# Twelve projection pairs by seven products instead of nine, with plain pairs taken one channel tile at a time

## The chip, the cores and the metric

The kernel runs on one core of one Trainium2 chip. The core has a matmul engine (PE, with its weight loads listed as PEld), VectorE (DVE), ScalarE (ACT), GpSimd (POOL) and SyncE (SP), which here only issues transfers. The metric is the device time of one execution in microseconds. Before the change the median of 3 runs is 2563.29 us (2563.03 to 2566.54).

## What is computed

One layer of a bidirectional encoder on 1024 prompt tokens and 256 sample tokens with model width 2048:

```
h = rmsnorm(x, norm_w)
proj = h @ w_in                       # 9232 columns
na_q, na_k, na_v, na_g, ml_qk, ml_v, ml_o, ml_z, ml_gp = split(proj)
att = neighbourhood_attention(na_q, na_k, na_v, na_rpb) * silu(na_g)   # 8 heads of 128
qk  = silu(centred_depthwise_conv(ml_qk, conv_w, conv_b))
h   = bidirectional_mlstm(*split(qk), ml_v, ml_gp + gate_b)            # 4 heads of 256
mem = rmsnorm(h, head_norm_w) * sigmoid(ml_o) * silu(ml_z)
y   = rmsnorm(x + concat(att, mem) @ w_out, final_norm_w)
```

All of it is float32. The kernel keeps that precision with three matmuls for each product: both operands are split into a high and a low part (ScalarE writes the high part, VectorE the difference), and high times high, high times low and low times high are added up in PSUM.

## The kernel before

**Tokens and channels.** The 1280 tokens fall into group A (768) and group B (512, half of them the sample's). The projection's channels are counted in tiles of 128; two neighbouring tiles are a *pair*, named by its first tile: q is 0 to 7 (`QT0`), k 8 to 15 (`KT0`), the attention's gate 16 to 23 (`GT0`), the mLSTM's q and k 24 to 39 (`QK0`), its output gate 40 to 47 (`OT0`), its z gate 48 to 55 (`ZT0`), and from 56 on v in eight units. The inner dimension has 16 blocks of 128.

**Stage one** (from 0 to about 1097 us) does every pair for group A. `first_tiles` takes tiles 0 to 3 plainly; then `pair_a` goes through the list `order` (lines 591 to 594), which begins with pairs 4 and 6. Each pair is a product of 2x2 blocks by Strassen's seven products in Winograd's form, 168 matmuls of 384 columns. GpSimd makes four sums of weight blocks for it (`summed`, line 512), and for a pair in `SECOND` these sums are also written to a scratch tensor `sD` (line 526), 16 writes of 128 KB. While a pair's matmuls run, `bg` is stepped: the end of the pair before (`finish_a`), which scales, splits, convolves or applies a tanh and stores.

**Stage two** begins with v units 4 and 0 and plain pair 0 for group B. Then `pair_s` (line 1342) does the nine pairs in `SECOND` by seven products for group B: 168 matmuls of 256 columns (line 1379), with the four sums read back from `sD`. All other pairs of group B are done by `proj_pair` (line 650): 96 matmuls of 512 columns (line 662) over two PSUM banks at once, in four steps of one 512 KB load, two splits and 24 matmuls; and v by `proj_v` (line 718), 192 matmuls of 256 columns (line 740) into two banks, or four "a" banks for unit 4.

**Attention and mLSTM** are written as generators. `run` steps two streams in turn at high priority: the mLSTM's units and, for each head, `na_sample`, then `na_prompt` with a setup and four blocks. The plain pairs and v units, listed ahead of it in the code at ordinary priority, and then four `late_gate` calls (two pairs each, for output gate and z gate) supply matmuls in between. What each head reads (`qS`, `kS`, `vS`) goes through scratch tensors in HBM, so a head can start only when its q, k and v have been projected and stored.

**The order on each engine** is made when the program is built: a list scheduler with a simulated timeline takes instructions by priority and readiness and hands out buffers of a ring in turn. On the chip each engine then runs its list in that order, so an instruction whose operand is late holds up all that follow it on its engine. SP's queue of transfers is such a list as well.

**Rings that the change touches.** PSUM has eight banks: three under the tag "pr", five under "a" (`bank`, line 73). In SBUF, `na_sample` loads a sample's q and k into the tile "nqk" (line 797), of which there is one and which `na_prompt`'s setup also uses for 2 MB of a prompt's q and k (lines 844 and 845); "hf" is a ring of eight that holds the mLSTM's operands (line 764); "sml" is a ring of six (line 770).

**The output stage** begins when the mixed heads are in HBM: 32 loads of 320 KB (`mix_block`, line 1492, on GpSimd's queue) go into SBUF that attention's pool gave back, and seven products in each of two halves give the output.

Of the kernel before, what the change touches and what calls it, by code (L numbers as in the profile page):

```python
# [8 lines left out]
F32 = mybir.dt.float32  # L9
F32R = mybir.dt.float32r  # L10
# [28 lines left out]
    GT0, QK0 + 8, GT0 + 2, QK0, KT0, GT0 + 4, KT0 + 2, GT0 + 6, KT0 + 4,  # L39
)  # L40
# [5 lines left out]
def kernel(  # L46
# [26 lines left out]
    def bank(tag, name):  # L73
        return ps.tile([P, 512], F32, tag=tag, name=name, bufs=3 if tag == "pr" else 5)
# [207 lines left out]
    def first_tiles():  # L282
        names = ("pr", "pr", "pr", "a", "a", "a", "a", "a")
# [184 lines left out]
    def pair_a(n1, bg=iter(()), hook=None):  # L468
        nm = f"A{n1}"
        tags = ("pr", "pr", "pr", "a", "a", "a", "a")  # L470
# [120 lines left out]
    order = [4, 6]  # L591
    rest = list(range(KT0, QK0, 2)) + list(range(OT0, NCH, 2))
# [57 lines left out]
    def proj_pair(n1, X, late=False):  # L650
        pb = [bank("pr", f"pc{n1}_{j}") for j in range(2)]
        for r in range(4):
            raw = w_piece(w_in[n1 // 2, r], f"{n1}_{r}")
            t = [w_split(raw, j * 512, j * 512 + 512, f"{n1}_{r}{j}") for j in range(2)]
            for f_ in range(2):
                for q in range(2):
                    xs = X.get(8 * f_ + 2 * r + q)
                    c = (2 * f_ + q) * P
                    first, last = r + f_ + q == 0, r == 3 and f_ == 1 and q == 1
                    for j, passes in enumerate((FORTH, FORTH[::-1])):  # L660
                        for m, (wi, xi) in enumerate(passes):
                            PE.matmul(  # L662
                                pb[j], t[j][:, wi, c : c + P], xs[xi],
                                start=first and m == 0, stop=last and m == 2,
                            )
        out = []
        for j in range(2):
            o = po(f"pco{n1}_{j}")
            if QK0 <= n1 < OT0:
                ct = n1 - QK0 + j  # L670
                DM.dma_start(o[:, 0:4], qb[ct])
                for z in (260, 518):
# [3 lines left out]
                    pb[j].rearrange("p (s c) -> p s c", s=2),  # L676
# [6 lines left out]
            out_scaled(o, pb[j], rbs[1], n1)  # L683
# [25 lines left out]
    def proj_v(u, X):  # L709
# [54 lines left out]
    def sml(name, n=256, dt=F32):  # L764
        return ap.tile([P, 260], dt, tag="sml", name=name, bufs=6)[:, :n]
# [29 lines left out]
    def na_sample(h):  # L795
        nm = f"nas{h}"
        qk = na_tile("nqk", [P, 4, TP], f"{nm}qk", 1, F32R)[:, :, :TS]
# [26 lines left out]
        b = bank("a", f"{nm}o")  # L824
# [625 lines left out]
    for i, n in enumerate(SECOND):  # L1450
        bg = pair_s(n, ("pr", "a")[i % 2], bg)
# [328 lines left out]
```

## Time and profile before

| | us |
|---|---|
| median of 3 runs | 2563.29 |
| the profiled execution, own time | 2565.18 |
| its span | 2563.3 |
| mean granted clock of the matmul engine | 0.997 |
| stage one | about 0 to 1097 |
| seven-product pairs of stage two | 1173 to 1350 |
| attention, mLSTM, plain pairs | 1350 to 2114 |
| plain pairs alone | 2114 to 2160 |
| output stage | 2160 to 2563 |

How to read the profile: every time is in microseconds from the start of the span unless it is marked ns. A row of busy times names engine, time, share and number of instructions. A row of waits names who waited at which line, for whom, for how long in total, how often, and the longest. A row of the chain names start, duration, engine, tile and line; "L662 x158" is 158 instructions of line 662 in one piece. A row of a group of instructions names line, engine, operation, tile written from tiles read, shape and count, then busy time and mean ns of one, then idle time of the engine ahead of them and what ended it. In a row of a single tile the three numbers are shortest, median and longest duration in ns, followed by first and last start. Names have their numbers left out where they differ only by them: "nap3qk" is the q and k of head 3's prompt, "nas3qk" those of its sample, "S32bx" a PSUM bank of seven-product pair 32 and "pc" one of a plain pair. "busy" of the matmul engine is modelled: matmuls overlap, so a mean duration is longer than the step from one start to the next.

### The profile page before, as it was taken

To read this page: it belongs to the slowest core of one execution; us is meant where nothing else is said; L and a number is where in the kernel's file an instruction comes from. 1 tells how busy PE (TensorE), PEld (TensorE's weight loads), DVE (VectorE), ACT (ScalarE), POOL (GpSimd) and SP (SyncE) were. 2 spreads that over 40 slices of the span, in tenths; PEclk is the share of its full clock that TensorE was granted. 3 is DMA by queue.
4 is the path that set the end of the run, shared out by engine and by line. 5 is a ranking of instruction groups with operands and counts; after the bars stand their busy time and mean duration, and the time that the engine had idled before them with its cause. 6 is when DMAs were issued, how large, how long until landed. Compare 5 with 4: busy or idle time off the path is not lost.

```text
span 2563.3 us, 44540 instructions
## 1 busy us (share of the span) xinstructions
PE 2534.0 (99%) x15054; PEld 2368.6 (92%) x15054; DVE 1972.6 (77%) x4029; ACT 1345.0 (52%) x3041; POOL 615.3 (24%) x909
## 2 busy tenths in 40 slices
PE   8999999999999999999999999999999999999998
PEld 8999999999999999999999999998988887788886
DVE  8769888888869798898875866765855665879695
ACT  8535545444444444465655666655745543344444
POOL 0535555444544444410001110100100104000001
PEclk9999999999999999999999999999999999999999
DMA  6546464536434342467768878877867849636237
GB/s 215 174 143 200 143 199 130 179 124 200 125 112 126 101 141 89 154 228 223 239 223 299 297 243 272 293 234 261 286 197 251 277 126 377 202 125 218 85 87 254
DMA packets 303483, 503.03 MB, mean 196 GB/s; under 512 B 48752, under 2 KB 191256, under 8 KB 303256
## 3 DMA queue, kind: packets, MB, share of 16 engines
q1 hardware_dynamic: 299096, 484.46, 58.9%
q0 software_dynamic: 4160, 15.73, 1.6%
q8 instruction: 119, 1.95, 0.3%
q14 instruction: 108, 0.88, 0.1%
HBM read 373.13 MB, written 126.95 MB: 195 GB/s over the span
## 4 chain that ended last, share of the span: by engine, by line
PE 92%; DMA 5%; DVE 2%; issue 1%; ACT 1%; SPq 0%; POOL 0%; ACTq 0%; POOLq 0%; DVEq 0%
PE pc L662 16%; PE po L1613 14%; PE pv L740 5%; PE fb L274 2%; PE A24b L274 1%; PE A12b L274 1%; PE A16b L274 1%; PE A44b L274 1%; PE A48b L274 1%; PE A52b L274 1%; PE A40b L274 1%; PE A20b L274 1%; PE A8b L274 1%; PE A50b L274 1%; PE A42b L274 1%; PE A22b L274 1%
## 5 line engine op out<-in xcount | busy, mean ns | idle before, releaser
L1613 PE MATMUL po<-wo,mo 128*128 128x512 f32 x1620 | 376.9, 393 | 3.7 <-ACT wo L165 2.8
L1613 PEld LDWEIGHTS po<-wo,mo 128*128 128x128 f32 x1620 | 303.6, 188 | 76.2 <-ACT wo L165 4.2
L166 DVE TENSOR_TENSOR ws<-wr,ws 128x512 fp32r<-128x512 f32 x152 | 104.3, 696 | 53.2 <-ACT ws L165 52.4
L165 ACT CAST ws<-wr 128x512 fp32r<-128x512 f32 x152 | 92.5, 617 | 70.1 <-PE pc L662 57.5
L165 ACT CAST mo<-mb 128x640 fp32r<-128x640 f32 x72 | 51.8, 726 | 92.5 <-PE po L1613 73.7
L116 POOL TENSOR_SCALAR rs<-rs 128x1 f32<-128x1 f32 x10 | 3.4, 341 | 351.2 <-DVE rs L1593 351.1
L166 DVE TENSOR_TENSOR mo<-mb,mo 128x640 fp32r<-128x640 f32 x72 | 59.1, 827 | 27.1 <-ACT mo L165 27.0
L1562 DVE TENSOR_TENSOR y<-y,po 128x512 f32<-128x512 f32 x90 | 58.5, 687 | 11.3 <-PE po L1613 11.0
L165 ACT CAST mo<-ms 128x640 fp32r<-128x640 f32 x40 | 28.9, 726 | 61.1 <-PE po L1613 32.1
L166 DVE TENSOR_TENSOR wsv<-wr_v,wsv 128x512 fp32r<-128x512 f32 x64 | 44.4, 700 | 14.2 <-ACT wsv L165 13.9
L165 ACT CAST wsv<-wr_v 128x512 fp32r<-128x512 f32 x64 | 39.0, 617 | 26.8 <-PE pv L740 15.5
L1576 ACT ACTIVATE jk<-y 128x512 f32<-128x512 f32 x40 | 25.2, 631 | 36.5 <-DVE y L1562 36.2
L413 DVE SCALAR_TENSOR_TENSOR pcv<-pco,cw_sb,pcv 128x516 f32<-128x516 f32 x48 | 36.7, 764 | 7.1 <-ACT pcv L407 7.0
L166 DVE TENSOR_TENSOR mo<-ms,mo 128x640 fp32r<-128x640 f32 x40 | 32.8, 823 | 7.6 <-ACT mo L165 7.6
L129 ACT ACTIVATE xq<-xq 128x1024 f32<-128x1024 f32 x20 | 21.2, 1061 | 31.7 <-DMA xq<-in_xtok_dram 29.2
L1081 POOL MEMSET mls_0v<- 128x2 f32 x4 | 0.4, 102 | 145.1 <-DVE S_dt.float L166 119.7
L274 PE MATMUL fb<-xg,fw 128*128 128x384 f32 x192 | 34.6, 334 | 0.0
L251 DVE TENSOR_TENSOR pco<-pc,rstdb 128x512 f32<-128x512 f32 x30 | 20.6, 687 | 17.8 <-PE pc L662 17.1
L274 PEld LDWEIGHTS fb<-xg,fw 128*128 128x128 f32 x192 | 33.4, 188 | 0.0
L778 DVE CUSTOM_DVE_ANT_0 nap_0st<-nap_0s,nap_0bt 128x384 f32<-128x384 f32 x32 | 17.7, 555 | 20.1 <-PE nap_0s L773 8.7
L1525 DVE TENSOR_TENSOR ms<-mb,mb 128x640 f32<-128x640 f32 x40 | 32.8, 823 | 0.0
L1492 POOL DMA_DIRECT2D mb<-mx x32 | 17.7, 554 | 58.8 <-DVE ws L166 24.8
(2655 smaller groups left out, 8512.4 us busy)
## 6 DMA issues: line engine op xcount, KB each, us to landing
wr<-in_w_in_dram SPq DMA_DIRECT2D x76, 512.0 KB, 4.7
wr_v<-in_w_in_dram SPq DMA_DIRECT2D x32, 512.0 KB, 5.0
wb<-in_w_o_dram SPq DMA_DIRECT2D x48, 256.0 KB, 3.0
xq<-in_xtok_dram SPq DMA_DIRECT2D x20, 512.0 KB, 4.2
mb<-mx POOLq DMA_DIRECT2D x32, 320.0 KB, 8.2
wr_wp<-in_w_o_dram SPq DMA_DIRECT2D x16, 512.0 KB, 4.0
vS<-vo SPq DMA_DIRECT2D x24, 256.0 KB, 5.1
nap_0bt<-in_rpb_tab_dram SPq DMA_DIRECT2D x32, 192.0 KB, 4.3
```

The costliest lines, as they stand in the source:

```text
L129: S.activation(raw, raw, AF.Square, accum_out=ssq[g][:, t, q : q + 1])
L165: S.copy(hi, src)
L166: V.tensor_tensor(lo, src, f(hi), op=ALU.subtract)
L251: V.tensor_tensor(o, src, rb, op=ALU.mult)
L274: PE.matmul(o, w(a_), x(b_), start=first and m == 0, stop=last and m == 2)
L413: V.scalar_tensor_tensor(dst[:, a:n], src[:, a + j - pad : n + j - pad], cw_sb[:, ct, j : j + 1], dst[:, a:n], op0=ALU.mult, op1=ALU.add,)
L662: PE.matmul(pb[j], t[j][:, wi, c : c + P], xs[xi], start=first and m == 0, stop=last and m == 2,)
L740: PE.matmul(outs[tt], xs[:, tt * P : (tt + 1) * P], t[:, wi, q * w : (q + 1) * w], start=first and m == 0 and (gates or tt % 2 == 0), stop ...
L1525: V.tensor_tensor(t, x, y_, op=op)
L1562: V.tensor_tensor(Y[p, q, tt], Y[p, q, tt], bk, op=op)
L1576: S.activation(jk, Y[p, q, tt], AF.Square, accum_out=ss[t][:, c : c + 1])
L1613: PE.matmul(bk[tt], m[xi][:, tt * P : (tt + 1) * P], w[wi], start=first and kk == 0 and j == 0, stop=last and j == 2, skip_group_check=True,)
```

## The change

Three more pairs are added to `SECOND`: k pair 14 and q pairs 4 and 6. They are thereby spilled in stage one, done by `pair_s` in stage two, and left out of the plain pairs.

```diff
 SECOND = (
     GT0, QK0 + 8, GT0 + 2, QK0, KT0, GT0 + 4, KT0 + 2, GT0 + 6, KT0 + 4,
+    KT0 + 6, QT0 + 4, QT0 + 6,
 )
```

Stage one opens with two output-gate pairs (40, 42); pairs 4 and 6 come to the head of the rest, which are dealt out two at a time behind an mLSTM pair and a v pair.

```diff
-    order = [4, 6]
-    rest = list(range(KT0, QK0, 2)) + list(range(OT0, NCH, 2))
+    order = [OT0, OT0 + 2]
+    rest = [4, 6] + list(range(KT0, QK0, 2)) + list(range(OT0 + 4, NCH, 2))
```

One of the three "pr" banks becomes a bank "m". It serves where the third "pr" bank served in `first_tiles`, `pair_a`, `pair_s` and the output stage, takes the first tile of plain pair 0, and holds the outputs of attention, which were in the "a" ring.

```diff
-        return ps.tile([P, 512], F32, tag=tag, name=name, bufs=3 if tag == "pr" else 5)
+        return ps.tile([P, 512], F32, tag=tag, name=name, bufs={"pr": 2, "m": 1, "a": 5}[tag])
...
-        bg = pair_s(n, ("pr", "a")[i % 2], bg)
+        bg = pair_s(n, (("pr", "pr", "m"), ("a", "a", "a"))[i % 2], bg)
...
-        b = bank("a", f"{nm}o")
+        b = bank("m", f"{nm}o")
...
-            b = bank("a", f"{n2}o")
+            b = bank("m", f"{n2}o")
```

A plain pair runs through the whole inner dimension for its first channel tile, scales and stores it, and then does the second. A load brings the weights of one tile for two of the four steps.

```diff
     def proj_pair(n1, X, late=False):
-        pb = [bank("pr", f"pc{n1}_{j}") for j in range(2)]
-        for r in range(4):
-            raw = w_piece(w_in[n1 // 2, r], f"{n1}_{r}")
-            t = [w_split(raw, j * 512, j * 512 + 512, f"{n1}_{r}{j}") for j in range(2)]
...
         out = []
         for j in range(2):
+            pb = bank("m" if n1 + j == QT0 else "pr", f"pc{n1}_{j}")
+            for r in range(4):
+                if r % 2 == 0:
+                    raw = w_piece(
+                        w_in[n1 // 2, r : r + 2, :, j * 512 : (j + 1) * 512].rearrange(
+                            "r p c -> p r c"
+                        ),
+                        f"{n1}_{j}{r}",
+                    )
+                t = w_split(raw, r % 2 * 512, r % 2 * 512 + 512, f"{n1}_{j}{r}")
+                for fq in range(4):
+                    f_, q = divmod(fq, 2)
+                    xs = X.get(8 * f_ + 2 * r + q)
+                    first, last = r + fq == 0, r + fq == 6
+                    for m, (wi, xi) in enumerate(FORTH[:: (1, -1)[fq % 2]]):
+                        PE.matmul(
+                            pb, t[:, wi, fq * P : fq * P + P], xs[xi],
+                            start=first and m == 0, stop=last and m == 2,
+                        )
             o = po(f"pco{n1}_{j}")
```

The v units' splits out of PSUM get high priority. In attention and mLSTM, a sample's q and k come into a buffer of the ring "hf", "sml" has seven buffers, and the throw-away output of the squares has a buffer of its own.

```diff
-            store_v(u, GA + tt * P, o, outs[tt][:, :256], rc[:, tt : tt + 1])
+            with tc.high_priority():
+                store_v(u, GA + tt * P, o, outs[tt][:, :256], rc[:, tt : tt + 1])
...
-        return ap.tile([P, 260], dt, tag="sml", name=name, bufs=6)[:, :n]
+        return ap.tile([P, 260], dt, tag="sml", name=name, bufs=7)[:, :n]
...
-        qk = na_tile("nqk", [P, 4, TP], f"{nm}qk", 1, F32R)[:, :, :TS]
+        qk = hf(f"{nm}qk")[:, : 4 * TS].rearrange("p (i c) -> p i c", i=4)
...
-                jk = sml(f"{n2}jk{e}")
+                jk = ap.tile([P, 256], F32, tag="jk", name=f"{n2}jk{e}", bufs=1)
```

More of the change, by code (lines that the diff above doesn't have):

```diff
@@ L650, in proj_pair @@
     def proj_pair(n1, X, late=False):
-        pb = [bank("pr", f"pc{n1}_{j}") for j in range(2)]
-        for r in range(4):
-            raw = w_piece(w_in[n1 // 2, r], f"{n1}_{r}")
-            t = [w_split(raw, j * 512, j * 512 + 512, f"{n1}_{r}{j}") for j in range(2)]
[L655 to L665, printed above, removed]
         out = []
         for j in range(2):
+            pb = bank("m" if n1 + j == QT0 else "pr", f"pc{n1}_{j}")
[17 more added lines that the diff above has]
+                        )
             o = po(f"pco{n1}_{j}")
@@ L1340, with pair_s @@
     BLOCK = {1: 0, 2: 1, 4: 3}
-    def pair_s(n1, tag, bg):
+    def pair_s(n1, tags, bg):
         nm = f"S{n1}"
-        bx, by, bz = (bank(tag, f"{nm}b{i}") for i in "xyz")
+        bx, by, bz = (bank(t, f"{nm}b{i}") for t, i in zip(tags, "xyz"))
         x0, y0, z0, y1, z1 = bx[:, :256], by[:, :256], bz[:, :256], by[:, 256:], bz[:, 256:]
@@ L1644, in product @@
             each(tt)
-    slots = iter(("aaaaa" "ppp") * 8)
+    slots = iter((("a",) * 5 + ("pr", "pr", "m")) * 8)
     def p_banks(p, j):
-        return [bank("pr" if next(slots) == "p" else "a", f"po{p}_{j}_{i}") for i in range(NT)]
+        return [bank(next(slots), f"po{p}_{j}_{i}") for i in range(NT)]
     for i in range(4):
```

8 lines of the change are left out of this document (4 added, 4 removed).

## The prediction

> **What bounds the kernel now.** I read the page's busy times first, then the waits of the matmul engine, then busy times by stretch, and for the terms of the sum the chain in order of time.
>
> ```profile
> span 2563.3 us, 44540 instructions
> PE 2534.0 (99%) x15054; PEld 2368.6 (92%) x15054; DVE 1972.6 (77%) x4029; ACT 1345.0 (52%) x3041; POOL 615.3 (24%) x909
> ```
>
> The matmul engine is busy for all but 29.3 us. So an edit counts if it shortens the stream of matmuls or one of the few places where that stream stands still. Those are, waits first and then stretches (columns: PE, PEld, DVE, ACT and POOL busy, granted clock, DMA share, GB/s):
>
> ```profile
> PE fb L274 <- ACT fw L172: 7.1, 1, 7.1
> PE nap_0s L773 <- DMA nap3qk<-kS: 2.5, 1, 2.5
> PE nap_0s L773 <- DMA nap4qk<-kS: 1.9, 1, 1.9
> PE A4b L274 <- DVE A4s L173: 1.7, 1, 1.7
> PE A6b L274 <- ACT A4c L483: 1.5, 1, 1.5
> PE nap_0s L773 <- DMA nap2qk<-kS: 0.5, 1, 0.5
> ```
>
> ```profile
> 1173.00:1350.00 177.00, 177.00 (x1538) 176.50 (x1537) 140.26 (x274) 105.54 (x203) 0.39 (x6) 1.00 0.72 227
> 1350.00:2113.60 763.60, 758.49 (x4833) 687.75 (x4832) 513.20 (x1396) 448.57 (x1114) 68.59 (x252) 1.00 0.78 254
> 2113.60:2160.20 46.60, 46.60 (x202) 37.77 (x202) 25.38 (x39) 15.20 (x25) 20.11 (x37) 1.00 0.94 364
> 2160.20:2201.00 40.80, 37.09 (x156) 28.59 (x154) 27.68 (x42) 12.61 (x21) 8.53 (x16) 1.00 0.89 325
> ```
>
> The first stretch is the nine seven-product pairs of stage two; the second is attention and mLSTM with plain pairs between their matmuls; the third is plain pairs alone; the fourth is the start of the output stage, where 3.7 us are lost.
>
> **Three more seven-product pairs.** From the chain in order of time (start, us, what):
>
> ```profile
> 1195.47 2.84 PE S32bx L1379 x24
> 1234.05 2.84 PE S24bx L1379 x24
> ...
> 1892.00 36.60 PE pc L662 x158
> ...
> 2101.31 6.11 PE pc L662 x26
> ...
> 2113.64 39.53 PE pc L662 x170
> ```
>
> Two pairs by seven products, 32 and 18, lie between 1195.47 and 1234.05: 19.29 us each. A plain matmul takes 36.60/158 = 0.2316 or 39.53/170 = 0.2325 us; 96 of 0.232 make 22.27 us. Three pairs move from the second form to the first: 3 x (22.27 - 19.29) = **8.9 us** less on the engine that sets the end. The break-even pace of a 256-column matmul is 22.27/168 = 0.133 us; the rows show 19.29/168 = 0.115.
>
> The Trainium skill, TensorE: Matmul & The Clock Gate, Back-to-back issue gap, speaks against narrow products: it gives a sustained pace of about 131 ns at 512 columns and 81 ns at 128, from which I estimate some 98 ns at 256, so 16.4 us for seven products against 12.6 us plain, and three pairs would cost 12 us. The trace's 0.232 us at 512 columns contradicts this; the same section's isolated gap (N/2.4 + 2.5 ns) would make the saving 7.1 us.
>
> Each moved pair needs 14 splits of 128x512 in stage two instead of 8, and its sums and folds beside them:
>
> ```profile
> L166 DVE TENSOR_TENSOR ws<-wr,ws 128x512 fp32r<-128x512 f32 x152 | 104.3, 696 | 53.2 <-ACT ws L165 52.4
> L165 ACT CAST ws<-wr 128x512 fp32r<-128x512 f32 x152 | 92.5, 617 | 70.1 <-PE pc L662 57.5
> ```
>
> That is 6 x 0.696 = 4.2 us more for VectorE and 6 x 0.617 = 3.7 us more for ScalarE per pair, in a stretch where VectorE has 36.7 of 177 us free and the matmul engine shows none. The two q pairs also write 256-byte runs from there instead of later; as many packets as before, and the DMA share is 0.72. Cost nothing; without that cover 3 x 4.2 = 12.6 us at most.
>
> The pairs' operand sums are spilled in stage one: 16 writes per pair on the SP queue, each waiting for GpSimd's sum, with the next weight load and the stores of the pair before queued behind it.
>
> ```profile
> 211.48 9.36 PE A8b L274 x54
> 271.21 29.13 PE A26b L274 x168
> 801.56 9.36 PE A44b L274 x54
> 861.29 29.13 PE A36b L274 x168
> sD<-A8t SPq DMA_DIRECT2D x16, 128.0 KB, 2.2
> ```
>
> Pairs 8 and 10 spill and split k: 271.21 - 211.48 = 59.73 us. Pairs 44 and 46 do neither: 861.29 - 801.56 = 59.73 us. So 48 more spills cost nothing, and pairs 4 and 6 where 40 and 42 stood cost nothing either, their stores being of the kind that 8 and 10 make.
>
> **The opening.** Pairs 40 and 42 take the place of 4 and 6. The two waits there (1.7 and 1.5 us) are for the splits of the opening's own tiles and for the copy that follows, and those stay. Zero, between -3.2 and 0; the lighter end of pair 40 (a tanh in place, two stores) gives no reason for a loss.
>
> **Plain pairs one tile at a time, and the PSUM banks.** 96 matmuls, 8 splits and 4 loads per pair, as before; a load now brings two runs of 2 KB for a partition instead of one of 4 KB, and feeds 24 matmuls as before.
>
> ```profile
> wr<-in_w_in_dram SPq DMA_DIRECT2D x76, 512.0 KB, 4.7
> L251 DVE TENSOR_TENSOR pco<-pc,rstdb 128x512 f32<-128x512 f32 x30 | 20.6, 687 | 17.8 <-PE pc L662 17.1 <-DMA mlp_2k<-cS 0.7
> L168 ACT ACTIVATE vo<-pv,rstdc x32: 454/472/505, 1120.5 to 1862.3; 128x256 fp32r<-128x256 f32 x32
> L169 DVE SCALAR_TENSOR_TENSOR vo<-pv,rstdc,vo x32: 462/481/491, 1122.7 to 1863.7; 128x256 fp32r<-128x256 f32 x32
> ```
>
> A bank lasts half a pair, 11 us, and is emptied in 0.69 us beside the next one's matmuls. With two "pr" banks instead of three the tight place is behind a v unit: it holds both, and the next unit's first matmul waits until two tiles have been split out of the older one, 2 x (0.472 + 0.481) = 1.9 us, covered by the v unit's last 12 matmuls and by attention. Six v units in the second stretch: 0 to 11.4 us; I take 1, since attention's matmuls stand next in the engine's order and the change gives these splits priority.
>
> **Sample q and k from the other ring.** Now a sample's q and k use the only buffer of the prompt's. Head 3:
>
> ```profile
> L773 PE MATMUL nap_1s<-nap2qk x12: 334/335/342, 1555.2 to 1595.3; 128*128 128x384 f32 x12
> L799 SPq DMA_DIRECT2D nas3qk<-kS x1: 606/606/606, 1596.2 to 1596.2; - x1
> L773 PE MATMUL nas_1s<-nas3qk x3: 274/277/279, 1619.5 to 1619.7; 128*128 128x256 f32 x3
> L845 SPq DMA_DIRECT2D nap3qk<-kS x1: 602/602/602, 1624.0 to 1624.0; - x1
> L773 PE MATMUL nap_0s<-nap3qk x12: 333/337/421, 1634.4 to 1688.1; 128*128 128x384 f32 x12
> ```
>
> The prompt's last score ends at 1595.3, the sample's load goes out at 1596.2, its scores end at 1619.7, and only then, at 1624.0, goes the next prompt's load, for which the matmul engine stands until 1634.4. After the change that load can go out 27.8 us sooner, behind the last score of the prompt before, and 10.4 us are all it took. The three waits (2.5 + 1.9 + 0.5 = 4.9 us) lose their cause, and so does what follows two of them:
>
> ```profile
> 1634.40:1640.00 5.60, 5.60 (x32) 5.56 (x33) 4.00 (x12) 2.13 (x7) 1.77 (x6) 0.70 1.06 385
> 1734.00:1740.00 6.00, 6.00 (x35) 6.00 (x36) 3.33 (x11) 2.84 (x9) 0.60 (x1) 0.72 0.97 330
> ```
>
> The granted clock is 0.70 and 0.72 there: 0.30 x 5.6 + 0.28 x 6.0 = 3.4 us. Together 8.3; I take **6**, since the order of matmuls is laid down ahead by a planner and another load can be the late one (bounds -8.3 and 0).
> The Trainium skill, same page, Part 1 on the clock gate, has the clock halve after an idle window of about 3.4 us; here waits of 2.5 and 1.9 us were enough, so by the page's figure the term would be at most 4.9 instead of 8.3, and the rows decide.
>
> The sample takes one of the eight "hf" buffers of the mLSTM for about 20 us per head; bounded by nothing (a free one) and the mLSTM's next unit 20 us later, hidden as long as plain pairs remain. One more "sml" and a buffer of its own for the squares' output only loosen. The single "m" bank for attention's outputs leaves all five "a" banks to the rest.
>
> **What is late next.** The second stretch loses 66.8 us of plain matmuls, and attention must still end ahead of them. Today it ends at 2113.6 and 46.6 us of plain pairs follow. Attention lost about 30 us at 1892 (158 plain matmuls in a row take 36.6 us, where a stretch like the one at 2101 has 6), waiting for the last q and k pairs; and
>
> ```profile
> L799 SPq DMA_DIRECT2D nas4qk<-kS x1: 567/567/567, 1691.4 to 1691.4; - x1
> L799 SPq DMA_DIRECT2D nas4qk<-qS x1: 524/524/524, 1714.6 to 1714.6; - x1
> ```
>
> head 4's q came 23.2 us after its k, from a plain pair as well. All three pairs involved (4, 6, 14) are then done before attention starts. Without any shortening of the heads, attention takes 763.6 - 30 = 734 us of the 763.6 + 46.6 - 66.8 = 743 that the engine needs; with 10 us less in each of seven heads, some 664. So the matmul engine stays the bound, and about 80 us of plain pairs follow attention. Then the output stage's loads, whose start is set by attention's end, are further along when the stage begins: the 3.7 us lost there shrink to nothing or, with no lead left (46.6 us more of the same loss, 3.71/40.8 each), grow by 4.2. I take -1.
>
> **Sum**, against the profiled execution's own time, 2565.2 us (span 2563.3 and 1.9 around it): -8.9 - 6 + 1 - 1 = -14.9, so 2550.3. That execution lies 1.9 us above the median of the three runs, 2563.3, so a median near **2548**.
>
> **The rivals.** (a) The products are saved and the waits come back elsewhere: other loads late, clock dips with them. For it: the transfers run at a DMA share of 1.0 and the planner did not foresee them. Against: the shared buffer is gone. 2563.3 - 8.9 = 2554. (b) What is won is lost at the banks and at the output stage, both terms at their bad ends: -8.9 - 6 + 11.4 + 4.2 = +0.7, so 2564. For it: a bank less for the plain pairs. Against: no wait for a bank among the matmul engine's waits today. (c) Attention ends last. It decides from the point where it takes over 743 us. Held up 5% by the "hf" ring it shares and the one "m" bank: 734 + 37 = 771, so 28 us of idle engine, and 4.2 more in the output stage: 2563.3 - 8.9 + 28 + 4 = 2586, **slower**. For it: only 9 us to spare if the heads get no shorter. Against: the load that ended each head's pause moves ahead by 28 us. (d) Narrow products run at the break-even pace or worse: no gain from them, 2557 with the other terms. Against: every row of the stretch.
>
> **How the numbers follow.** Forecast 0.61 (its own range 2541 to 2552), (a) 0.20, (b) 0.08, (c) 0.09, (d) 0.02. What a measurement of this kernel can tell from no change is 0.2%, 5.1 us: faster is below 2558.2. The forecast and (a), with half of (d), give faster 0.82; (b) and the rest of (d) same 0.09; (c) slower 0.09. The low end has every term at its good bound, -8.9 - 8.3 - 3.2 - 3.7 = -24.1, so 2539; the high end takes in (a) and the milder half of (b), 2562.
>
> **What would show it.** Seven-product pairs every 19.3 us, twelve times; no wait of the matmul engine for a prompt's q and k; the granted clock at 1.00 from 1400 to 2150; plain matmuls alone for more than 46.6 us before the output stage; its start without the 3.7 us. I am wrong if the matmul engine idles ahead of attention's last units, if waits stand behind v units, or if stage one's pairs exceed 59.7 us for two.

## The result, and the profile after

The changed kernel takes 2572.09 us (median of 7 runs, 2567.87 to 2577.93), the kernel before on the same chip 2562.7 us (7 runs, 2559.49 to 2566.54): ratio 1.0039, 95% interval 1.0028 to 1.0050. It is slower by 0.39%; 2548 was forecast, and the range ended at 2562.

The profiled execution after took 2572.09 us itself; that of before lies 2.5 us above the median of this comparison. The head of the page, and the waits of the matmul engine (us in total, times, longest):

```profile
span 2570.4 us, 45222 instructions
PE 2533.5 (99%) x15270; PEld 2376.0 (92%) x15270; DVE 1989.5 (77%) x4062; ACT 1353.2 (53%) x3071; POOL 611.1 (24%) x909
```

```profile
PE fb L275 <- ACT fw L173: 6.9, 1, 6.9
PE mlp0a3tb L1126 <- DMA mlp0a3cv<-cD: 2.3, 1, 2.3
PE mlp3a2kv L1101 <- POOL mlp3a0v L1089: 2.3, 1, 2.3
...
PE mls_0s L1101 <- DMA mls_0q<-cS: 2.0, 2, 1.8
...
PE pc L669 <- DVE vo L170: 1.2, 1, 1.2
PE mlp_3in L1101 <- DVE mlp_1zr L1286: 1.2, 1, 1.2
```

The three waits for a prompt's q and k are gone, and there is a longer list in their place; behind the first row no single wait is longer than 2.3 us. The stretches (the columns as in the prediction):

```profile
1176.40:1411.00 234.60, 234.60 (x2041) 234.16 (x2040) 181.19 (x347) 137.61 (x266) 0.26 (x4) 1.00 0.73 227
1411.00:1450.00 39.00, 34.08 (x248) 32.23 (x247) 16.68 (x52) 15.88 (x43) 5.49 (x27) 0.91 0.98 312
1905.00:1940.00 35.00, 29.22 (x206) 27.09 (x206) 22.15 (x67) 17.70 (x50) 2.97 (x15) 0.95 0.82 259
1411.00:2079.40 668.40, 653.62 (x4353) 599.96 (x4352) 466.04 (x1330) 412.24 (x1059) 70.49 (x252) 0.99 0.83 268
2079.40:2170.00 90.60, 90.60 (x393) 73.50 (x393) 42.37 (x64) 26.44 (x44) 23.16 (x42) 1.00 0.73 255
2170.00:2210.80 40.80, 40.13 (x173) 31.88 (x171) 28.11 (x43) 14.35 (x23) 5.49 (x10) 1.00 0.88 315
```

Stage two runs as computed: no idle time in 234.6 us, 57.6 us more than the first row of before for three more pairs, 19.2 each. The stretch of attention has 668.4 - 653.6 = 14.8 us of idle matmul engine where before had 763.60 - 758.49 = 5.1. Two places hold most of it: the first 39 us lose 4.9 idle and 0.09 x 39 = 3.5 to the lower clock, the 35 us at 1905 lose 5.8 and 1.8.

What such a wait looks like at 1906 (start, us, engine, line, tiles, count; in brackets the idle time ahead and what ended it):

```profile
1906.25 0.28 PE L745 MATMUL pv<-wsv,x_4h 128*128 128x256 f32 x1
1908.29 1.66 PE L1101 MATMUL mls_0s<-mls_0q,mls_0k 128*128 128x256 f32 x12 [1.75 <-DMA mls_0q<-cS]
...
1911.94 0.28 PE L745 MATMUL pv<-wsv,x_4h 128*128 128x256 f32 x1
```

The engine stands for a load of the mLSTM's q, while the matmul of a v unit that comes at 1911.94 is the next of the 24 that share one piece of split weights with the one at 1906.25 (19 had run): it was ready, and stood further down in the order.

One measure serves for all kernels below. From the trace: the time from each matmul's start to the next one's, less the median for its column count, added up where the excess is over 60 ns, from the last matmul of stage two to the first of the output stage. It holds idle time and low clock together and is called **pauses**. Every kernel has 9 to 12 us of it in pieces under 0.1 us; what differs is the rest. It is taken from one execution of each kernel, and two executions of one kernel differ in time by several us (the changed one by 10), so small differences of pauses say little. In the table "to output stage" runs from the end of stage two to the first matmul of the output stage, and "output stage" to its last matmul, with 9.0 to 9.4 us behind it.

```
us                        stage two   its     to output   pauses  plain     output  span
                          starts at   length  stage       in it   at its end stage
before                    1173.3      176.6   810.1       17.7    46.4      393.9   2563.3
after                     1176.5      234.4   759.2       33.0    90.7      391.3   2570.4
```

So the account of the two profiled executions: stage two starts 3.2 later; +57.8 in it; the stretch to the output stage would shrink by three plain pairs, 66.8, and shrinks by 50.9, because pauses grow by 33.0 - 17.7 = **15.3**; the output stage gives 2.6 back. 3.2 + 57.8 - 50.9 - 2.6 = +7.5, and 7.1 is the difference of the spans (0.4 less lies behind the last matmul). Plain matmuls of 512 columns still start every 0.232 us, so the saving by the products, 57.8 - 66.8 = -9.0, is there in full; the pauses eat it and more.

### The profile page after: what moved, and what is told of

The parts are those of the page before. It is cut to its first block, busy times and chain, and to the rows that moved or that the text cites. A ratio compares the mean times of both kernels' runs of the same rounds, so it can differ in the third digit from the quotient of the medians.

```text
span 2570.4 us, 45222 instructions
## 1 busy us (share of the span) xinstructions
PE 2533.5 (99%) x15270; PEld 2376.0 (92%) x15270; DVE 1989.5 (77%) x4062; ACT 1353.2 (53%) x3071; POOL 611.1 (24%) x909
## 5 line engine op out<-in xcount | busy, mean ns | idle before, releaser
L166 ACT CAST ws<-wr 128x512 fp32r<-128x512 f32 x128 | 78.3, 616 | 93.3 <-PE pc L669 61.3
L167 DVE TENSOR_TENSOR ws<-wr,ws 128x512 fp32r<-128x512 f32 x128 | 87.7, 689 | 49.5 <-ACT ws L166 48.0
L1569 DVE TENSOR_TENSOR y<-y,po 128x512 f32<-128x512 f32 x90 | 58.2, 680 | 11.3 <-PE po L1620 11.0
L1499 POOL DMA_DIRECT2D mb<-mx x32 | 17.7, 554 | 76.4 <-DMA mx<-pco 41.4
```

Source lines behind the costliest of these rows:

```text
L166: S.copy(hi, src)
L167: V.tensor_tensor(lo, src, f(hi), op=ALU.subtract)
L1499: G.dma_start(t, mixT[8 * kh + kk][:, th * TH : (th + 1) * TH])
L1569: V.tensor_tensor(Y[p, q, tt], Y[p, q, tt], bk, op=op)
```

## First experiments: undo a part of the change

Three theories. R: the sample's q and k in the mLSTM's ring hold up the mLSTM's loads. D: with three plain pairs fewer, the same transfers of attention come closer together and late. B: the pauses come from the banks and from going one tile at a time. All ratios below are to the kernel before on the same chip, with their 95% intervals.

**Nine pairs in the changed kernel.**

```diff
 SECOND = (
     GT0, QK0 + 8, GT0 + 2, QK0, KT0, GT0 + 4, KT0 + 2, GT0 + 6, KT0 + 4,
-    KT0 + 6, QT0 + 4, QT0 + 6,
 )
```

> The changed kernel with nine seven-product pairs, all its other edits kept. Theory R (ring: the sample's q and k in the mLSTM's ring of eight, and the prompt's 2 MB load that is thereby let go early, make other loads late): the new waits stay and 8.9 us of matmuls come back, about 2581 us. Theory D (density: with three plain pairs fewer between them, attention's and the mLSTM's loads follow each other faster and come late in any ring): the waits go, 2555 to 2563. Theory B (banks: two banks and one tile at a time hold the plain pairs up): about 2581.

Measured: 2568.63 us, 1.0027 (1.0017 to 1.0038), pauses 21.1. No theory gave this: R and B stood at 2581, D at 2563 or less. The other edits together cost 0.27% with nine pairs, and the last three pairs another 0.12%, which these intervals do not tell from nothing, where they should have saved 0.35%.

**Twelve pairs in the kernel before, nothing else**, the three pairs of the diff above added to its nine.

> The kernel before with the twelve pairs alone; opening, banks, plain pairs and rings as before. R and B: the 8.9 us are kept, about 2554. D: late loads in the stretch of attention as in the changed kernel, 2565 to 2572.

Measured: 2589.35 us, 1.0109 (1.0094 to 1.0124), pauses 35.4. The pairs alone, in the order of the change, are the most costly version of all, far over what any theory gave (R and B 2554, D up to 2572). Its longest wait, and two stretches, the plain pairs behind attention and the start of the output stage:

```profile
PE po L1614 <- issue: 11.8, 1, 11.8
```

```profile
2145.60:2173.40 27.80, 16.05 (x70) 12.69 (x69) 9.75 (x17) 7.17 (x12) 11.27 (x21) 0.83 1.00 359
2173.40:2214.20 40.80, 35.34 (x132) 27.84 (x133) 21.45 (x32) 9.10 (x14) 14.25 (x26) 0.87 1.01 387
```

With only 27.8 us between attention's end and the output stage the transfers run at a share of 1.0 and the engine stands for 11.8 us, for which the profile names no cause; that it is the loads of the output stage is a reading. The output stage as a whole takes 404.6 us against 391 to 394 where 46 us or more lie between.

**The sample's q and k back in the prompt's buffer**, otherwise the changed kernel.

```diff
-        qk = hf(f"{nm}qk")[:, : 4 * TS].rearrange("p (i c) -> p i c", i=4)
+        qk = na_tile("nqk", [P, 4, TP], f"{nm}qk", 1, F32R)[:, :, :TS]
```

> The changed kernel with the sample's q and k back in the prompt's buffer. R: the new waits (some 20 us with their clock dips) go and the old ones (some 8) come back, about 2560. D and B: about 2572, or up to 8 more.

Measured: 2578.27 us, 1.0059 (1.0046 to 1.0072), pauses 40.2. Theory R falls for this kernel: without the ring it is slower.

**Plain pairs two tiles at a time again, three pr banks, attention's outputs in the a banks**, otherwise the changed kernel.

```diff
-        return ps.tile([P, 512], F32, tag=tag, name=name, bufs={"pr": 2, "m": 1, "a": 5}[tag])
+        return ps.tile([P, 512], F32, tag=tag, name=name, bufs=3 if tag == "pr" else 5)
...
+        pb = [bank("pr", f"pc{n1}_{j}") for j in range(2)]
...
-        b = bank("m", f"{nm}o")
+        b = bank("a", f"{nm}o")
```

> The changed kernel with plain pairs two tiles at a time, three pr banks, and attention's outputs in the a banks, as before. B: about 2560. R and D: about 2572.

Measured: 2580.93 us, 1.0070 (1.0057 to 1.0083). Theory B falls. Pauses are 28.6 here, under the 33.0 of the changed kernel; the loss is at the output stage, 409.7 us, with 27.9 us of plain pairs ahead of it. So in this kernel one tile at a time earns its place by ending attention sooner.

## Second: places and transfers

Theory O: the loss at the start of attention comes from a q pair in the last place of stage two.

**Pair 12 last again.**

```diff
-    GT0, QK0 + 8, GT0 + 2, QK0, KT0, GT0 + 4, KT0 + 2, GT0 + 6, KT0 + 4,
+    GT0, QK0 + 8, GT0 + 2, QK0, KT0, GT0 + 4, KT0 + 2,
     KT0 + 6, QT0 + 4, QT0 + 6,
+    GT0 + 6, KT0 + 4,
```

> The changed kernel with the twelve pairs in another order: pairs 14, 4 and 6 come ahead of 22 and 12, so that pair 12 ends stage two, as in the kernel before. Theory O (the border): a q pair in the last place puts its stores and the 2 MB load of head 0 on the SP queue ahead of the mLSTM's first loads, and the matmul engine idles 4.9 us in the 39 us behind stage two and runs 3.5 us slower under a granted clock of 0.91. Then those 39 us keep all of their matmul time and clock, and the time falls by 6 to 8 us from 2572, to about 2565. Theory D (density: with three plain pairs fewer, the same transfers of attention and mLSTM must come in 51 us less): the loss only moves to another load, time within 3 us of 2572.

Measured: 2561.53 us, 1.0007 (0.9999 to 1.0016): the order of the list alone is worth 0.32%, 8 us, as theory O said. But the place is only half right. Its first stretch, beside 1411.00:1450.00 of the changed kernel:

```profile
1408.70:1448.00 39.30, 36.94 (x275) 35.35 (x275) 19.07 (x59) 18.12 (x49) 3.12 (x17) 0.96 0.96 334
```

Idle 2.4 instead of 4.9, clock 0.96 instead of 0.91: pauses there 4.7 against 9.7 us, 5.0 less, and some 2 us less elsewhere. Nor is the reason the one that was given. The SP queue of the changed kernel, then of this one (start, us it took to issue):

```profile
1411.84 0.37 SPq L196 DMA_DIRECT2D qS<-S_dt.float  x1
1412.32 0.59 SPq L1078 DMA_DIRECT2D mls_0k<-cS  x1
...
1419.58 0.71 SPq L851 DMA_DIRECT2D nap0qk<-kS  x1
...
1423.97 1.08 SPq L1072 DMA_DIRECT2D mlp0a3cv<-cD  x2
```

```profile
1408.80 0.33 SPq L218 DMA_DIRECT2D kS<-S_dt.float32r  x1
...
1409.71 0.58 SPq L1079 DMA_DIRECT2D mls_0k<-cS  x1
...
1417.31 0.52 SPq L852 DMA_DIRECT2D nap0qk<-kS  x1
...
1422.49 2.87 SPq L1073 DMA_DIRECT2D mlp0a3cv<-cD  x2
```

The loads stand in the same order, but for two that here go ahead of `mlp0a3cv` (`nas_1bt` and `mlp0a2v`), and the first leaves 1.4 us behind the end of stage two with the q pair's stores and 1.0 without. What differs is the order of matmuls around them: in the changed kernel they come to `mlp0a3cv` at 1431.1, 20.2 us after stage two, and stand until it has landed at 1433.4; here they come to it 24.7 us after stage two and do not wait. That the list's order matters is shown; the stores as its cause are not.

**Stage one opened by pairs 4 and 6 again**, with twelve pairs.

```diff
-    order = [OT0, OT0 + 2]
-    rest = [4, 6] + list(range(KT0, QK0, 2)) + list(range(OT0 + 4, NCH, 2))
+    order = [4, 6]
+    rest = list(range(KT0, QK0, 2)) + list(range(OT0, NCH, 2))
```

> The changed kernel with stage one opened by pairs 4 and 6 again, 40 and 42 back in their old places; nothing else. The prediction put this edit at 0 (-3.2 to 0). If it is free, the time stays within 3 us of 2572 and stage two starts within 1.5 us of 1176.5. If the opening with output-gate pairs is what makes stage two start 3 us later than before, it starts at about 1173.5 and the time falls to about 2569.

Measured: 2576.12 us, 1.0065 (1.0053 to 1.0078), 0.26% over the changed kernel; stage two starts at 1178.0. Neither guess, within 3 us of 2572 or about 2569, came out. With 4 and 6 among the twelve, opening with them puts their 32 spills into the start, and the engine loses in the 390 us behind it. The same stretch of this kernel, then of the changed one:

```profile
110.00:500.00 390.00, 387.82 (x2245) 386.07 (x2244) 323.80 (x602) 189.17 (x460) 198.14 (x210) 1.00 0.59 181
```

```profile
110.00:500.00 390.00, 389.65 (x2254) 387.23 (x2252) 320.42 (x596) 189.83 (x459) 189.96 (x212) 1.00 0.57 173
```

Idle 2.2 against 0.4 us; the kernel before, which opens with 4 and 6 but does not spill them, idles 1.5 there. All three kernels with twelve pairs and the old opening start stage two at 1178.0 to 1179.4. So the new opening is no loss; it avoids one that comes with these two pairs at the start, and the spills are the likely reason.

**Ten pairs in the changed kernel**: the three lines of the list end in `KT0 + 2, KT0 + 6, GT0 + 6, KT0 + 4`.

> The changed kernel with ten seven-product pairs (only pair 14 is added to the nine, pair 12 last). Theory D: a pair's saving of 3 us is given back only where attention's transfers run short, so ten is at or a little under nine pairs in this frame (2568.6 there): 2564 to 2568, and between stage two and the output stage the matmul engine idles 8 to 12 us. Theory O: with pair 12 last the border is clean and each pair saves its 3 us: 2565.6. If each pair costs about 1 us whatever its place (3.5 us for three), the time is 2570.

Measured: 2570.88 us, 1.0042 (1.0029 to 1.0056), pauses 24.4. Theory O's 2565.6 fails, and so does D's 2568 at most: with pair 12 last ten pairs are no faster than nine (1.0027) in this kernel. The third guess, that each pair costs about 1 us, gave 2570 and is nearest.

**Half of the plain pairs' weight bytes left out**, otherwise the changed kernel: `w_half` loads 256 KB where `w_piece` loaded 512 KB, and both k rows are split from one half, so those channels get other values.

```diff
-                    raw = w_piece(
-                        w_in[n1 // 2, r : r + 2, :, j * 512 : (j + 1) * 512].rearrange(
...
+                    raw = w_half(w_in[n1 // 2, r, :, j * 512 : (j + 1) * 512], f"{n1}_{j}{r}")
-                t = w_split(raw, r % 2 * 512, r % 2 * 512 + 512, f"{n1}_{j}{r}")
+                t = w_split(raw, 0, 512, f"{n1}_{j}{r}")
```

> The changed kernel with half of the weight bytes of the plain pairs left out (a 256 KB load for each 512 KB one; both k rows are then split from the same half, so those channels of the output are other values; matmuls, splits and stores are the same in number and size). Theory D: the losses between stage two and the output stage (idle 14.8 us, 5.1 us under a lower clock) are transfers that come late because the DMA engines are 85 to 87% busy there; with some 5 MB less they shrink to 8 or less, and the time to 2560 or less. Theory O, or the planner's order: the losses stay above 15 us and the time above 2566.

Measured: 2566.11 us, 1.0033 (1.0020 to 1.0045), not to be told from the changed kernel's 1.0039. The stretch of attention, beside 1411.00:2079.40 above, and the waits that it now has:

```profile
1408.20:2076.10 667.90, 656.44 (x4370) 602.25 (x4369) 467.85 (x1336) 415.96 (x1062) 69.14 (x252) 0.99 0.78 250
```

```profile
PE mlp0a3tb L1126 <- DMA mlp0a3cv<-cD: 2.3, 1, 2.3
...
PE mlp_3tp L1272 <- DVE mlp_3hs L1270: 1.6, 2, 1.5
...
PE mlp_1in L1101 <- DVE nap_0pt L799: 1.2, 1, 1.2
PE mlp_1in L1101 <- ACT mlp_1x L1230: 1.0, 1, 1.0
```

The share of the DMA engines falls from 0.83 to 0.78, the late load of `mls_0q` is gone but for 0.2 us, that of `mlp0a3cv` stays, and waits for VectorE and ScalarE have come: pauses 27.9. Theory D, in the form that transfers are too dense, falls.

## Third: one part alone on the kernel before

Theory P is the prediction's: the ring removes waits and nothing takes their place. Theory M: the waits move to the mLSTM's units.

**The ring alone**, with the line of the third experiment changed the other way.

> The kernel before with one edit of the change alone: a sample's q and k in the mLSTM's ring of eight hf buffers instead of the prompt's nqk buffer. The prediction put it at -6 (bounds -8.3 and 0). Theory P (as predicted): the three waits for a prompt's q and k (4.9 us) and the low clock behind them go, nothing comes in their place: 2554 to 2557 against a kernel before of about 2560 to 2562. Theory M (the waits move): with the prompt's loads early, attention no longer sets the pace, the mLSTM's units come closer together and wait for their own q, k and buffers: the nqk waits go, but the sum of pauses of the matmul engine longer than 60 ns between stage two and the output stage stays at 15 to 21 us (17.7 before), and the time stays within 3 us of before.

Measured: 2567.83 us, 1.0024 (1.0015 to 1.0033), pauses 19.2 against 17.7. Its waits:

```profile
PE mlp_2s L1095 <- DVE mlp_0zr L1280: 2.0, 1, 2.0
PE mlp_2s L1095 <- DVE nap_0pt L793: 1.9, 2, 1.7
...
PE mlp_0in L1095 <- ACT mlp_0x L1224: 1.6, 1, 1.6
PE mlp0a3kv L1095 <- issue: 1.2, 1, 1.2
```

The waits for q and k (4.9 us) are gone and 6.7 us of others have come, 5.5 of them for results of VectorE and ScalarE and 1.2 without a named cause; none of the four is for a load. Theory P falls, and M's pauses are right; but M gave 3 us at most, and the median is 5.9 higher. The profile's stages show 2.8 of that (spans 2566.1 and 2563.3), most of it ahead of stage two. The rest stays open.

**One tile at a time and the banks alone**: `proj_pair`, the bank counts and the tags as in the change, the rest as before.

> The kernel before with another part of the change alone: plain pairs one channel tile at a time, two pr banks, one m bank, attention's outputs in it, five a banks left. The prediction put it at +1 (0 to 11.4). If it only costs what was worked out, 0 to 3 us slower than before. Theory M needs no part of it: the nqk waits stay, within 3 us of before. If this part makes the mLSTM's new small waits, the sum of pauses over 60 ns between stage two and the output stage rises from 17.7 to 25 or more and the time by 6 us or more.

Measured: 2559.93 us, 0.9991 (0.9982 to 0.9999), pauses 12.6. Here too the waits for a prompt's q and k have vanished from the list, although sample and prompt still share their buffer:

```profile
PE pc L668 <- DVE vo L169: 1.9, 2, 1.1
...
PE mlp_3in L1099 <- ACT mlp_3x L1228: 0.5, 1, 0.5
```

The 1.9 us behind v units are what the prediction looked for, and they cost less than what goes away. The shared buffer was a place where before's order stood still, not a necessity. Theory M's guess for this run, that the waits for q and k stay, fails with it.

**The twelve pairs with 12 last, ring undone; and without the priority.** The first takes the diff of the third experiment, the second drops `with tc.high_priority():`.

> The twelve pairs with 12 last (run e5_last), with the sample's q and k back in the prompt's nqk buffer. Theory M: with the ring undone the mLSTM's small waits shrink and the waits for a prompt's q and k come back, sum of pauses within 5 us of e5_last's 26.1, time within 4 us of it. Theory P: the ring saves its 6 to 8 us here: slower by 6 or more than e5_last.

> The twelve pairs with 12 last (run e5_last), without the priority given to the splits that empty a v unit's two banks. If the priority does its work, the matmul engine waits behind v units for a pr bank: up to 1.9 us for each of the six v units between stage two and the output stage, so 5 to 11 us slower. If the priority is what pushes the mLSTM's own work on VectorE and ScalarE back (waits for mlp tiles), the time falls by 3 us or more. If neither, within 3 us.

Measured: 2564.42 us, 1.0013 (1.0004 to 1.0021), pauses 24.1; and 2562.38 us, 1.0004 (0.9996 to 1.0013), pauses 21.1. Both within 3 us of the twelve pairs with 12 last: on that kernel neither the ring nor the priority can be told from nothing. The second also shows how far pauses can be trusted: without the priority the matmuls run in the same order (5 of 15270 places differ by name), the time is the same, and yet pauses are 21.1 against 26.1. So 5 us of pauses between two single executions can be chance, or at least no difference in time.

## Fourth: the pairs on a calm kernel

Theory A: a pair saves 3.0 us wherever nothing else is new. Theory C: each plain pair taken out takes 22 us of cover from the chains of attention and mLSTM. All four are the kernel with one tile at a time (0.9991), and the list has pair 12 last.

```diff
# ten
+    GT0, QK0 + 8, GT0 + 2, QK0, KT0, GT0 + 4, KT0 + 2, KT0 + 6, GT0 + 6, KT0 + 4,
# twelve
+    GT0, QK0 + 8, GT0 + 2, QK0, KT0, GT0 + 4, KT0 + 2,
+    KT0 + 6, QT0 + 4, QT0 + 6, GT0 + 6, KT0 + 4,
# opening
+    order = [OT0, OT0 + 2]
# twelve and opening: both
```

> The plain-pair part alone (run e10_tiles, 0.9991 of before, pauses over 60 ns between stage two and the output stage 12.6 us) with a tenth seven-product pair, 14, and pair 12 last. Theory A (arithmetic: a pair saves 3.0 us where nothing else is new): 0.12% under e10_tiles, ratio about 0.998. Theory C (cover: each plain pair taken out of the attention stretch takes 22 us of cover from the chains of attention and mLSTM, which then show as pauses): pauses grow by 3 us or more, ratio 0.999 to 1.001.

> Run e10_tiles with twelve seven-product pairs, 14, 4 and 6 ahead of 22 and 12, no ring, no priority, the old opening. Theory A: 8.9 us under e10_tiles, ratio about 0.9956. Theory C: pauses between stage two and the output stage of 20 us or more against 12.6, ratio 0.999 to 1.002; and it takes the ring out of the question, since no sample uses the hf buffers here.

> Run e10_tiles with stage one opened by pairs 40 and 42. In the changed kernel, going back to 4 and 6 cost 0.26%. If that is the opening itself, this run is 2 to 6 us under e10_tiles (ratio 0.997 to 0.9985) and the matmul engine idles 1 to 3 us less ahead of stage two. If it was chance in the order laid down behind it, the ratio stays within 0.001 of 0.9991.

> Runs e14_twelve and e15_open together: the change without the ring, without the priority and with pair 12 last. If the parts add, the ratio is that of e14_twelve times that of e15_open over 0.9991. Theory A with a free opening: 0.995 to 0.996; Theory C: 0.998 to 1.001.

```
                     median us  ratio (95%)                pauses
ten                  2558.02    0.9987 (0.9978 to 0.9996)  13.3
twelve               2563.81    1.0009 (0.9999 to 1.0019)  23.4
opening              2559.14    0.9993 (0.9984 to 1.0002)  13.5
twelve and opening   2559.07    0.9988 (0.9979 to 0.9997)  20.4
```

With nine pairs the opening is worth nothing; with twelve it is worth 0.21%, which agrees with the spills as its reason. Theory A fails for twelve pairs, where theory C's numbers came out; for ten it is C that fails: it gave 3 us of pauses or more and a ratio of 0.999 at least, and neither is there, while A's 0.998 lies inside the interval. The stretch of attention with nine pairs, then with twelve, both with the new opening:

```profile
1349.60:2088.20 738.60, 735.35 (x4744) 668.90 (x4744) 504.96 (x1389) 441.97 (x1107) 67.85 (x252) 1.00 0.79 260
2088.20:2155.00 66.80, 66.80 (x289) 54.20 (x289) 31.54 (x48) 20.03 (x33) 22.61 (x41) 1.00 0.84 298
```

```profile
1410.30:2089.40 679.10, 671.57 (x4461) 617.05 (x4460) 480.71 (x1349) 423.69 (x1073) 67.10 (x252) 1.00 0.82 269
2089.40:2155.70 66.30, 66.28 (x287) 53.35 (x286) 30.28 (x46) 18.73 (x31) 23.17 (x42) 1.00 0.85 302
```

The same 66 us of plain pairs follow attention, so the three pairs were taken from between attention's matmuls: 738.6 becomes 679.1, and the idle time there 3.2 becomes 7.5. The like holds in all four places where twelve can be set against nine in the same code: pauses 12.6 to 23.4, 13.5 to 20.4, 21.1 to 33.0, 17.7 to 35.4 (11.9 of the last right ahead of the output stage), which is 7 to 18 us more against a saving of 8.9. Each is over the 5 us that can be chance, and all go one way. On the calm kernel part of the growth has a name: with nine pairs the matmul engine has no wait for a prompt's q and k there, with twelve these waits are back, 3.6 us in one kernel and 4.1 in the other. The tenth pair adds 0.7 us of pauses on the calm kernel and 3.3 in the changed one (21.1 to 24.4), neither to be told from chance. That is theory C as far as it goes, and it is a reading, not shown: eleven pairs were not tried, nor two others than 4 and 6, so it stays open whether it is the count or these two; and the next edit takes out no cover at all and adds 8.4 us.

**The same edit on two kernels.** One more sml buffer (`sml` is line 764 of the kernel before, `hf` line 758) and a buffer of its own for the squares' output add no work.

```diff
-        return ap.tile([P, 260], dt, tag="sml", name=name, bufs=6)[:, :n]
+        return ap.tile([P, 260], dt, tag="sml", name=name, bufs=7)[:, :n]
...
-                jk = sml(f"{n2}jk{e}")
+                jk = ap.tile([P, 256], F32, tag="jk", name=f"{n2}jk{e}", bufs=1)
```

> The kernel before with the two buffer edits that the prediction put at nothing (one more sml buffer, the squares' output in a buffer of its own). They add no work and take no buffer away, but the order laid down for the matmul engine changes behind them. Theory L (loosening only): ratio 0.999 to 1.001. Theory Z (any edit that lets the planner lay down another order moves the time by some 0.1 to 0.25%, since single pauses of 1 to 3 us come and go with it): outside 0.999 to 1.001, in either direction, with other groups among the waits for attention and mLSTM tiles.

> Run e16_both (0.9988 of before, pauses 20.4 us) with the same two buffer edits. Theory L: ratio 0.998 to 0.9995. Theory Z: outside of it. Together with e17_sml it says whether these edits have an effect of their own (the same sign and size in both) or only through the order (different).

Measured on the kernel before: 2558.53 us, 0.9993 (0.9984 to 1.0002), pauses 11.3 instead of 17.7, with the waits for a prompt's q and k gone here too. On twelve and opening: 2563.75 us, 1.0011 (1.0002 to 1.0020) instead of 0.9988, pauses 28.8 instead of 20.4. The second kernel's new waits:

```profile
PE mlp3a2kv L1100 <- issue: 2.5, 1, 2.5
PE mlp_3in L1100 <- DVE nap_1sm L787: 2.0, 1, 2.0
...
PE nap_0o L900 <- ACT nap_0os L897: 1.3, 1, 1.3
PE mls_0s L1100 <- DVE mlp_3hs L1259: 1.2, 1, 1.2
```

One way on one kernel (by less than can be told from nothing), 0.23% the other way on the other. Theory Z holds on the second: an edit without work of its own moves the time by two thirds of what was forecast for three pairs (0.23% against 0.35%). Another order of matmuls is laid down behind it, from the 9586th of 15270 on (on the kernel before from the 9108th of 15054); that this order is what costs the time is the likely reason, with no run that holds it fixed.

**From before to the changed kernel in single edits.** The runs make a ladder in which each row adds one edit to the row above:

```
                                             ratio    pauses
before                                       1        17.7
one tile at a time, banks                    0.9991   12.6
new opening                                  0.9993   13.5
twelve pairs, 12 last                        0.9988   20.4
the two buffer edits                         1.0011   28.8
priority of the v units' splits              1.0013   24.1
sample's q and k in the ring                 1.0007   26.1
q pair 6 last instead of 12: as changed      1.0039   33.0
```

Behind the first edit only two steps have intervals that lie apart: the buffers (0.23%) and the place of pair 12 (0.32%). The prediction put the buffers at nothing and did not look at the place. The three pairs give 0.05% here where 0.35% was forecast. What a step costs hangs on the kernel that it is made on: the ring adds 0.24% to the kernel before, nothing to be told here, and is a gain of 0.20% in the changed kernel.


## Why the prediction was wrong

**Right.** Twelve pairs at 19.2 to 19.5 us; the saving of 8.9, found as 9.0; stage one's pairs at 59.7 to 60.3 us for two behind the opening; no wait for a prompt's q and k; attention not the last to end, with 90.7 us of plain pairs behind it (about 80 were forecast); the output stage starting with 0.7 us idle instead of 3.7. One of its signs failed: the granted clock was to be 1.00 from 1400 to 2150, and is 0.91 and 0.95 in the two stretches above.

**The step that failed** is the term of -6 for the waits for a prompt's q and k, with its bounds of -8.3 and 0, and the nothing that stands beside it for what a new order costs in that stretch. The change of pauses there was **+15.3**. The prediction took "lose their cause" for "vanish" and gave the term no bad end: it named that another load could be late next, and closed the bounds at nothing. The ring alone shows it: 4.9 us of waits gone, 6.7 of others come, 0.24% slower (0.15% to 0.33%) instead of 0.23% faster. Nor was the shared buffer the whole cause of the waits: they are gone as well with one tile at a time alone, and with the two buffer edits alone, where sample and prompt still share it.

With it falls the sentence that with less filling the stretch shortens by the full 66.8 us because the matmul engine stays the bound. The engine is the bound at 99%, and still every pause in an order that is laid down ahead adds to the end, as at 1906, where it waits at the next matmul of its order while another further down is ready. Of the 15.3 us the other edits make 3.4 with nine pairs (17.7 to 21.1, no more than chance can make) and the three pairs 11.9 (21.1 to 33.0). About 7 of these 11.9 go with the place of the q pair (33.0 to 26.1 with 12 last); the rest is spread over waits of 1 to 3 us for loads, VectorE and ScalarE. Why just these orders make the engine wait more stays open.

**The rivals.** (a), waits that come back elsewhere, was the right mechanism; it was priced as if pauses stayed as they were (2554), where they grew by 15.3 us. (b) looked at the banks, and there was nothing: 1.2 us behind v units after, and that part alone is no loss. (c) gave the right sign for the wrong reason; attention ended 34 us sooner than before.

**Smaller terms.** The opening at 0 was right for that edit, but that 48 more spills cost nothing in stage one was right only with it: with 4 and 6 at the opening stage two starts up to 6 us later. Of stage two's start 3.2 us later in the changed kernel, 1.7 are 3.4 us at half the granted clock (96.2 to 99.6), which the kernel before does not have; the rest stays open, and the nine kernels with twelve pairs and the new opening start stage two anywhere from 1172.5 to 1176.5. The price of a short lead, 4.2 us, was too small: with 28 us of lead the output stage took 11 to 16 us more than before, and an 11.8 us wait stood ahead of it in one of the two kernels; both have two tiles at a time, and no run changes the lead alone; the changed kernel never came there.

**A version that beats both** is one tile at a time with ten pairs, or with twelve and the new opening, 12 last, and neither ring nor the extra buffers: 0.9987 and 0.9988, by about 3 us. That is less than the 0.2% named in the prediction. Both intervals lie under 1, but these are the best two of eighteen kernels, neither can be told from one tile at a time alone (0.9991), and the buffer edits took all of it away again on one of them.

## What to carry to other kernels

Where one engine is busy 99% of the time in an order that a planner lays down, count a saving in work as safe only in the stage that holds it; give the stretch whose filling it removes a bad end as well: here twelve pairs brought 7 to 18 us of pauses against 8.9 saved. When a wait loses its cause, ask which matmul then stands first in the order and what it needs. Measure an edit without work of its own on the same kernel before a few tenths of a per cent are put down to a part of the change.

## What the runs showed of the hardware that was not expected

The plain pairs' loads before, then after (KB, median us from issue to landing):

```profile
wr<-in_w_in_dram SPq DMA_DIRECT2D x76, 512.0 KB, 4.7
```

```profile
wr<-in_w_in_dram SPq DMA_DIRECT2D x64, 512.0 KB, 5.5
```

The same 512 KB took 0.8 us longer, in two runs of 2 KB for a partition instead of one of 4 KB; over the nineteen kernels with loads of this size the medians are 4.4 to 5.1 with runs of 4 KB (five kernels) and 5.1 to 5.8 with runs of 2 KB (fourteen). The prediction had named the runs and given them no price; the kernel with that part alone (5.2) is no slower for it (0.9991). Halving these bytes took the share of the DMA engines down by only 0.05 and left the time where it was.

Short pauses can cost more than their length, and not always. In the two kernels, up to the end of the output stage, low clock came in spells of 3.4 us, or twice that, at half the granted clock, so 1.7 us lost for each 3.4: before from 1635.7 to 1639.1 behind a wait of 2.5 us, after from 1434.2 to 1441.0 behind one of 2.3. With 12 last a wait of 2.8 us at 1906 had none behind it: the clock was 1.00 over the next 6 us.
